# Up projection of an MLP by seven products instead of eight: 26 pairs with ordinary tiles between their chunks, in place of 40 in a row

## The chip, the cores and the metric

One core of a Trainium2 chip runs the whole program. Its engines have separate in-order queues: TensorE (PE, matmuls; PEld are its weight loads), VectorE (DVE), ScalarE (ACT), GpSimd (POOL) and SyncE (SP, which here issues all DMAs). The metric is the device time of one execution in microseconds (us); lower is better.

## The reference

A decoder block on 512 tokens of width 2048 in float32: adaLN modulation, an RWKV-7 head group beside a pooling head group, an output projection with residual, then a gated MLP with a causal conv of width 3, residual, and a final RMSNorm. The part that matters here:

```python
def _conv_ffn(h, w_up, conv_w, conv_b, w_down):
    T = h.shape[1]
    u = h @ w_up
    up = jnp.pad(u, ((0, 0), (CONV_WIDTH - 1, 0), (0, 0)))
    y = conv_b
    for j in range(CONV_WIDTH):
        y = y + conv_w[j] * up[:, j:j + T]
    val, gate = jnp.split(y, 2, axis=-1)
    return (jax.nn.silu(gate) * val) @ w_down

        x = x + gt1 * mix
        h = _rmsnorm(x, norm2_g[l]) * (1.0 + sc2) + sh2
        x = x + gt2 * _conv_ffn(h, w_up[l], conv_w[l], conv_b[l], w_down[l])
    return _rmsnorm(x, norm_f_g)
```

`w_up` is 2048 x 11264 (44 tiles of 128 value columns and 44 of gate columns), `w_down` 5632 x 2048. `gt2`, the gate of the last residual, is one of six vectors `silu(c) @ w_ada + b_ada`.

## The kernel before

Activations lie transposed: channels on the 128 partitions, 512 tokens along the row. Every float32 product is made of three matmuls in a rounded format (`mm3`, L117): weights and activations are split into a high part (a cast, on ACT) and a low part (a subtraction, on DVE, or on POOL where a call says so), and high x high, high x low and low x high add up in one PSUM bank. `split_weights` (L107) loads a piece of 512 weight columns into a `wraw` buffer (four of them), casts it into `whi` (three) and subtracts into `wlo` (three); `project` (L122) runs a whole output tile so, in four pieces for 16 tiles of input channels. PSUM has eight banks (`bank`, L788).

The order of an engine's instructions is fixed before the run by a scheduler that models their times: of what is ready it takes what stands first in the program, so later work can come ahead of earlier work that waits. `tc.issue_after(x)` holds instructions behind `x` in the queue of its engine. A tile pool closed and opened again reuses the same memory, so a new tile waits for the readers of the old ones there.

The stages around the change:

- Output projection (L848 to L875): `x2` tiles are loaded, ten output tiles get their last two input tiles, six more run in two halves of 256 tokens; after each, `residual` (L803) adds into `x2` and its squares, and a store puts `x2[f]` to DRAM (`x2d`, L856 and L863), for the end of the kernel to read back (L1020).
- First up tiles (`up_first`, L824): pairs 0 and 1 of the up projection, value and gate tile each, over 16 input tiles, in two halves of tokens, while `second_norm` still makes the activations `H2`.
- `token_sums` (L905): for the products below, four combinations of token halves and input halves for each of eight pairs of `H2` tiles, 128 x 256 each: six additions or subtractions on POOL, then two casts (L919, ACT) and two subtractions (L920, DVE) into the tiles `tk`.
- Pairs 2 and 3 (`up_tile`, L927) as ordinary tiles: 16 x 3 matmuls with 512 columns of tokens each, 96 for a pair.
- Pairs 4 to 43 (`seven`, L937): a pair is seen as a 2 x 2 block product: token halves, halves of the input channels, and value or gate. Seven products of half-size blocks replace eight: 7 x 8 x 3 = 168 matmuls with 256 columns. The eight tiles of input come in four chunks. For a chunk, 512 KB of weights (four blocks) are loaded into `raw`; POOL makes four sums of blocks (L944 to L946); `parts` (L948) splits the three plain blocks and then the four sums into `uh` and `ul` (L954 on ACT, L955 on DVE); then 42 matmuls run, products 1, 2, 4 on plain blocks first, then 6, 7, 5, 3 on the sums. Each product has its own PSUM bank through the four chunks. At the end DVE combines the seven (L981 to L988) into value and gate.
- `gated` (L838): conv of value and gate (`conv`, L831: one pass of ACT, two of DVE each), silu, product, store to `actd`.
- Gate rows (`ada_gate2`, L994): beside pairs 4 to 35, two rows a pair: a 256 KB load and a DVE product with its sum (L1002) for `gt2`, 64 in all.
- Down projection (L1043 to L1074): 44 input tiles in steps of four over eight output tiles at a time, from reloaded `actd` tiles (L1031); the second eight output tiles end in two token halves.

Of the kernel before, what the change touches and what calls it, by code (L numbers as in the profile page):

```python
# [9 lines left out]
F32 = mybir.dt.float32  # L10
# [6 lines left out]
P = 128  # L17
T = 512
# [13 lines left out]
NORD = 4  # L32
# [29 lines left out]
def block_kernel(ctx, tc, a, out, stop=None, dbg=None):  # L62
# [43 lines left out]

    def split_weights(src, eng=V):  # L107
        w = src.shape[-1]
        raw = wp.tile([P, WC], F32, tag="wraw", name="wraw", bufs=4)
        nc.sync.dma_start(raw[:, 0:w], src)  # L110
        hi = wp.tile([P, WC], F32R, tag="whi", name="whi", bufs=3)
        S.copy(hi[:, 0:w], raw[:, 0:w])  # L112
        lo = wp.tile([P, WC], F32R, tag="wlo", name="wlo", bufs=3)
        eng.tensor_tensor(lo[:, 0:w], raw[:, 0:w], hi[:, 0:w].bitcast(F32), op=ALU.subtract)  # L114
        return hi, lo
# [721 lines left out]

    def gated(j, cv, cg):  # L838
        yv, yg = conv(cv, j, "t0"), conv(cg, 44 + j, "t1")
        S.activation(yg, yg, AF.Silu)  # L840
        after = V.tensor_mul(yv, yv, yg)
        nc.sync.dma_start(actd[j], yv)
        return after
# [8 lines left out]
    for f in range(NW):  # L852
        ps = bank()
        project(ps, a["wout"][f, :, NM * P :], M[NM:])
        residual(f, ps, mod[:, 32 + f : 33 + f], acc, 0, T, f == 0)
        nc.sync.dma_start(x2d[f], x2[f])  # L856
# [32 lines left out]
    for k in range(KT):  # L889
        up_first(1, k)  # L890
    rxctx.close()
# [13 lines left out]
    def token_sums(i):  # L905
        bb = up.tile([P, 2, T], F32, tag="raw", name="bb", bufs=3)
# [3 lines left out]
        tt = up.tile([P, 2, T], F32, tag="raw", name="tt", bufs=3)  # L910
# [4 lines left out]
        G.tensor_tensor(t4, t2, bb[:, 1, 0:HT], op=ALU.subtract)  # L915
        got = []
# [7 lines left out]
    for i in range(HK):  # L924
        token_sums(i)

    def up_tile(n):  # L927
        ps = bank()
        project(ps, a["wup"][n - 4, :, :], H2)
        return ps  # L930

    for j in range(2, NORD):
        gated(j, up_tile(2 * j), up_tile(2 * j + 1))
# [3 lines left out]
    def seven(j):  # L937
        q = {}
        for c in range(NPC):
            raw = up.tile([P, 4, W2], F32, tag="raw", name="raw", bufs=3)  # L940
            nc.sync.dma_start(raw, a["wups"][j - NORD, c, :, :, :])
            sm = [wp.tile([P, WC], F32, tag="wraw", name="sums", bufs=4) for _ in range(2)]
            sa, sb2 = (t[:, :].rearrange("p (n w) -> p n w", n=2) for t in sm)
            G.tensor_tensor(sa, raw[:, 1:3, :], raw[:, 0:1, :].to_broadcast([P, 2, W2]), op=ALU.add)  # L944
            G.tensor_tensor(sb2[:, 0, :], sa[:, 0, :], raw[:, 2, :], op=ALU.add)
            G.tensor_tensor(sb2[:, 1, :], sb2[:, 0, :], raw[:, 3, :], op=ALU.add)  # L946

            def parts(srcs):  # L948
                hi = up.tile([P, 4, W2], F32R, tag="uh", name="uh", bufs=3)
                lo = up.tile([P, 4, W2], F32R, tag="ul", name="ul", bufs=3)  # L950
                got, n = [], 0
                for t in srcs:
                    m = t.shape[1]
                    S.copy(hi[:, n : n + m, :], t)  # L954
                    V.tensor_tensor(lo[:, n : n + m, :], t, hi[:, n : n + m, :].bitcast(F32), op=ALU.subtract)  # L955
                    got += [(hi[:, n + i, :], lo[:, n + i, :]) for i in range(m)]
                    n += m
                return got

            a22, a11, a12 = parts([raw[:, 1:4, :]])  # L960
            s1, s3, s2, s4 = parts([sa, sb2])

            ks = [2 * c, 2 * c + 1]
            lo = [half([H2[k], H2[k + HK]], 0) for k in ks]
            hi = [half([H2[k], H2[k + HK]], 1) for k in ks]
            for n, w, xs_ in (
                (1, a11, [x[0] for x in lo]), (2, a12, [x[1] for x in lo]),
                (4, a22, [TK[k][3] for k in ks]), (6, s2, [TK[k][1] for k in ks]),
                (7, s3, [TK[k][2] for k in ks]), (5, s1, [TK[k][0] for k in ks]),
                (3, s4, [x[1] for x in hi]),  # L970
            ):
                if c == 0:
                    q[n] = bank()[:, 0:HT]
                for i in range(2):
                    sl = slice(i * P, (i + 1) * P)
                    mm3(q[n], w[0][:, sl], w[1][:, sl], *xs_[i], start=c == 0 and i == 0, stop=c == NPC - 1 and i == 1)
# [14 lines left out]
    cbs = []  # L991
    modg = cp.tile([P, 4, KT], F32, tag="modg", name="modg")

    def ada_gate2(n, after):  # L994
        kq, j = divmod(n, KT)
        if j == 0:
            cbs.append(wp.tile([P, WC], F32, tag="whi", name="cb2", bufs=3))
            nc.sync.dma_start(cbs[kq], cact[0:1, kq * T : (kq + 1) * T].partition_broadcast(P))
        wa = wp.tile([P, WC], F32, tag="wlo", name="wa3", bufs=3)
        nc.sync.dma_start(wa, a["ada3"][kq, j, :, :])  # L1000
        with tc.issue_after(after.ins):
            V.scalar_tensor_tensor(wa, wa, 1.0, cbs[kq], op0=ALU.mult, op1=ALU.mult, accum_out=modg[:, kq, j : j + 1])  # L1002

    for j in range(NORD, NF):
        after = gated(j, *seven(j))
        for n in range(2 * (j - NORD), 2 * (j - NORD + 1)):
            if n < 4 * KT:
                ada_gate2(n, after)
    upctx.close()
    V.tensor_add(modg[:, 0, :], modg[:, 0, :], modg[:, 1, :])  # L1010
    V.tensor_add(modg[:, 2, :], modg[:, 2, :], modg[:, 3, :])
    V.tensor_add(modg[:, 0, :], modg[:, 0, :], modg[:, 2, :])
    V.tensor_add(mod[:, 80:96], modg[:, 0, :], cols("b_ada", 80, 96))
# [28 lines left out]

    pss = [bank() for _ in range(NB)]  # L1043
    for k0 in range(0, NF, DK):
        A = act_tiles(k0)
        for f in range(NB):
# [31 lines left out]
def pack(x, c, w_ada, b_ada, norm1_g, w_in, mu_shift, w0, w2, a0, a2, g2, k_k, k_a, r_k, ln_x_w, ln_x_b,  # L1078
# [49 lines left out]
    def ftiles(w):  # L1128
# [53 lines left out]
```

## Time and profile before

| | us |
|---|---|
| median of three runs (lowest, highest) | 2409.46 (2406.38, 2413.34) |
| the profiled execution | 2411.78 |
| its span in the profile | 2409.9 |
| ordinary tiles of pairs 2 and 3, first matmul to first product | 45.2 |
| pairs 4 to 43, to the first matmul of the down projection | 859.7 |

The page gives for each engine its busy time and number of instructions, and then groups of instructions by line, with busy time, the mean of one, and what ended the idle time before. PE is busy 92% of the span, but its matmuls overlap in the pipeline, so that a busy time says less than the distance from one start to the next. Other views of the same trace give busy time by stage, the waits by pair of engines, and instructions in order of time.

### The profile page before, as it was taken

Reading aid. Unit: us, or ns where it says so; the run is one execution under the profiler, and the core shown is the slowest. Engines: PE = TensorE matmul, PEld = TensorE weight load, DVE = VectorE, ACT = ScalarE, POOL = GpSimd, SP = SyncE. Lnnn points to the kernel's source line nnn. Section 1 sums busy time; section 2 is a strip of 40 time slices with the busy share of each in tenths; the row PEclk is TensorE's granted clock in tenths of the full one; section 3 lists DMA queues with packets and bytes.
Section 4 is the critical chain, followed back from the end, with each engine's and each line's share of the span. In section 5 each row is a group of like instructions: output and inputs, shape, how many; then the busy total and the mean of one; then the engine's idle time right before and its main releaser. Section 6 shows DMA issues by size and latency. Waiting matters only on the chain.

```text
span 2409.9 us, 44500 instructions
## 1 busy us (share of the span) xinstructions
PE 2212.3 (92%) x17314; PEld 1923.0 (80%) x17314; DVE 1791.8 (74%) x2686; ACT 984.0 (41%) x1621; POOL 768.8 (32%) x558
## 2 busy tenths in 40 slices
PE   7998898898789797799999999999999999999997
PEld 5786656566567697699999999999999888888887
DVE  7896667576865469679999999999988633353357
ACT  4335242332423255344444444444444433343333
POOL 0000000000000016467778777787788300000000
PEclk9998999999989899799999999999999999999999
DMA  9884555547674664334334433443333554554455
GB/s 347 296 311 161 171 171 174 178 131 235 205 233 147 205 195 143 114 132 136 129 135 136 137 136 131 137 136 135 116 118 115 182 155 144 149 149 140 141 167 177
DMA packets 188837, 400.51 MB, mean 166 GB/s; under 512 B 36561, under 2 KB 48593, under 8 KB 184401
## 3 DMA queue, kind: packets, MB, share of 16 engines
q1 hardware_dynamic: 188626, 397.68, 50.6%
q8 instruction: 135, 2.21, 0.4%
q14 instruction: 76, 0.62, 0.1%
HBM read 363.51 MB, written 34.09 MB: 165 GB/s over the span
## 4 chain that ended last, share of the span: by engine, by line
PE 69%; DVE 13%; DMA 10%; issue 3%; ACT 2%; POOL 2%; SPq 1%; DVEq 0%; ACTq 0%; POOLq 0%
PE b L120 18%; PE b L118 17%; PE b L119 17%; DMA war<-ada 5%; DVE ul L955 3%; PE mm L120 3%; PE mm L118 3%; PE mm L119 3%; PE pf L118 2%; PE pf L119 2%; PE pf L120 2%; DVE wlo L114 1%; DVE war L369 1%; DVE t L834 1%; POOL bb L909 1%
## 5 line engine op out<-in xcount | busy, mean ns | idle before, releaser
L114 DVE TENSOR_TENSOR wlo<-wraw,whi 128x512 fp32r<-128x512 f32 (+1 forms) x466 | 324.8, 699 | 317.7 <-ACT whi L112 309.4
L112 ACT CAST whi<-wraw 128x512 fp32r<-128x512 f32 (+1 forms) x482 | 290.8, 606 | 562.4 <-PE b L119 255.2
L944 POOL TENSOR_TENSOR sums<-raw 128x512 f32<-128x512 f32 x160 | 324.4, 2028 | 185.0 <-DVE ul L955 151.1
L120 PE MATMUL b<-tk,ul 128*128 128x256 f32 x1280 | 366.0, 286 | 2.6 <-DVE ul L955 2.6
L118 PE MATMUL b<-ah,whi 128*128 128x512 f32 (+1 forms) x980 | 350.3, 357 | 14.6 <-ACT whi L112 13.6
L118 PE MATMUL b<-tk,uh 128*128 128x256 f32 x1280 | 362.1, 283 | 0.0
L119 PE MATMUL b<-tk,uh 128*128 128x256 f32 x1280 | 362.0, 283 | 0.0
L120 PE MATMUL b<-ah,wlo 128*128 128x512 f32 (+1 forms) x980 | 349.5, 357 | 5.6 <-DVE wlo L114 4.7
L119 PE MATMUL b<-al,whi 128*128 128x512 f32 (+1 forms) x980 | 348.6, 356 | 0.0
L120 PE MATMUL b<-hh,ul 128*128 128x256 f32 x960 | 274.9, 286 | 37.4 <-DVE ul L955 37.4
L955 DVE TENSOR_TENSOR ul<-sums,uh 128x512 fp32r<-128x512 f32 x320 | 288.9, 930 | 18.2 <-ACT uh L954 17.4
L118 PE MATMUL b<-hh,uh 128*128 128x256 f32 x960 | 271.6, 283 | 0.0
L119 PE MATMUL b<-hl,uh 128*128 128x256 f32 x960 | 271.5, 283 | 0.0
L955 DVE TENSOR_TENSOR ul<-raw,uh 128x768 fp32r<-128x768 f32 x160 | 246.5, 1541 | 13.3 <-ACT uh L954 13.2
L120 PEld LDWEIGHTS b<-tk,ul 128*128 128x128 f32 x1280 | 245.3, 192 | 5.8 <-DVE ul L955 4.2
L118 PEld LDWEIGHTS b<-tk,uh 128*128 128x128 f32 x1280 | 245.5, 192 | 0.0
L119 PEld LDWEIGHTS b<-tk,uh 128*128 128x128 f32 x1280 | 245.4, 192 | 0.0
L954 ACT CAST uh<-sums 128x512 fp32r<-128x512 f32 x320 | 182.7, 616 | 148.2 <-PE b L119 133.3
L118 PEld LDWEIGHTS b<-ah,whi 128*128 128x128 f32 x980 | 186.2, 190 | 43.0 <-ACT whi L112 17.1
L120 PEld LDWEIGHTS b<-hh,ul 128*128 128x128 f32 x960 | 184.0, 192 | 43.9 <-DVE ul L955 43.9
L120 PEld LDWEIGHTS b<-ah,wlo 128*128 128x128 f32 x980 | 186.1, 190 | 33.6 <-DVE wlo L114 6.6
L954 ACT CAST uh<-raw 128x768 fp32r<-128x768 f32 x160 | 132.8, 830 | 193.0 <-PE b L119 193.0
(265 smaller groups left out, 4468.5 us busy)
## 6 DMA issues: line engine op xcount, KB each, us to landing
raw<-wups SPq DMA_DIRECT2D x160, 512.0 KB, 3.2
war<-ada SPq DMA_DIRECT2D x96, 512.0 KB, 4.3
wraw<-wdn SPq DMA_DIRECT2D x192, 256.0 KB, 2.9
wa<-ada SPq DMA_DIRECT2D x32, 1024.0 KB, 7.8
wraw<-win SPq DMA_DIRECT2D x108, 256.0 KB, 3.9
ald<-actd SPq DMA_DIRECT2D x88, 256.0 KB, 2.7
wraw<-wout SPq DMA_DIRECT2D x78, 256.0 KB, 3.6
wa<-ada SPq DMA_DIRECT2D x64, 256.0 KB, 2.6
```

Source lines behind the costliest of these rows:

```text
L112: S.copy(hi[:, 0:w], raw[:, 0:w])
L114: eng.tensor_tensor(lo[:, 0:w], raw[:, 0:w], hi[:, 0:w].bitcast(F32), op=ALU.subtract)
L118: PE.matmul(ps, wh, xh, start=start, stop=False)
L119: PE.matmul(ps, wh, xl, start=False, stop=False)
L120: return PE.matmul(ps, wl, xh, start=False, stop=stop)
L369: V.scalar_tensor_tensor(wa, wa, 1.0, cq[0], op0=ALU.mult, op1=ALU.mult, accum_out=modq[:, kq, j : j + 1])
L834: V.scalar_tensor_tensor(y[:, 1:T], c[:, 0 : T - 1], col("cw", 88 + j), y[:, 1:T], op0=ALU.mult, op1=ALU.add)
L909: G.tensor_tensor(bb[:, q, :], hi[:, :].bitcast(F32), lo[:, :].bitcast(F32), op=ALU.add)
L944: G.tensor_tensor(sa, raw[:, 1:3, :], raw[:, 0:1, :].to_broadcast([P, 2, W2]), op=ALU.add)
L954: S.copy(hi[:, n : n + m, :], t)
L955: V.tensor_tensor(lo[:, n : n + m, :], t, hi[:, n : n + m, :].bitcast(F32), op=ALU.subtract)
```

## The change

Pairs 2, 3 and 4 are ordinary (`NORD` 5), pairs 5 to 30 are made by seven products (`NSEV` 26), and 31 to 43 are ordinary again. The tiles of these last thirteen are cut into quarters: a quarter (four input tiles, 12 matmuls) is run in each chunk of a product pair from the third chunk on, between the products on plain blocks and those on sums. Weight sums and the split of the plain blocks are made one chunk ahead; the split of the sums is queued behind the next chunk's plain split. Buffers of `raw`, `p` and `s` parts are two each. Sums' buffers lie in the memory of `wraw` and `wlo`.

Token sums: POOL's part of four is made at once, and the casts and subtractions stand behind the last weight split of an ordinary tile, one or two sums to a tile; POOL's part of the next sum follows each. The sixteen stores of `x2` come after the first up tiles. The gate rows move into the first pass of the down projection, eight rows in each of the steps two to nine, with two buffers of rows.

```diff
-NORD = 4
+NORD = 5
+NSEV = 26
...
-        S.copy(hi[:, 0:w], raw[:, 0:w])
+        mark[0] = S.copy(hi[:, 0:w], raw[:, 0:w]).ins
...
-        eng.tensor_tensor(lo[:, 0:w], raw[:, 0:w], hi[:, 0:w].bitcast(F32), op=ALU.subtract)
+        mark[1] = eng.tensor_tensor(lo[:, 0:w], raw[:, 0:w], hi[:, 0:w].bitcast(F32), op=ALU.subtract).ins
...
         residual(f, ps, mod[:, 32 + f : 33 + f], acc, 0, T, f == 0)
-        nc.sync.dma_start(x2d[f], x2[f])
...
-        if hf:
-            nc.sync.dma_start(x2d[f], x2[f])
...
         up_first(1, k)
+    for f in range(KT):
+        nc.sync.dma_start(x2d[f], x2[f])
     rxctx.close()
...
-        bb = up.tile([P, 2, T], F32, tag="raw", name="bb", bufs=3)
+        bb = up.tile([P, 2, T], F32, tag="raw", name="bb", bufs=2)
...
-        tt = up.tile([P, 2, T], F32, tag="raw", name="tt", bufs=3)
+        tt = up.tile([P, 2, T], F32, tag=("sh", "sl")[i % 2], name="tt", bufs=2)
...
-    for i in range(HK):
-        token_sums(i)
...
+    tts = [token_sums(i) for i in range(4)]
+    at = 0
     for j in range(2, NORD):
-        gated(j, up_tile(2 * j), up_tile(2 * j + 1))
+        tiles = []
+        for i in range(2):
+            ps = bank()
+            last = project(ps, a["wup"][2 * j + i - 4, :, :], H2)
+            tiles.append(ps)
+            for _ in range((1, 1, 2, 1, 2, 1)[2 * j + i - 4]):
+                with tc.issue_after(mark[0]), tc.issue_after(mark[1]):
+                    token_split(at, tts[at])
+                at += 1
+                if at + 3 < HK:
+                    tts.append(token_sums(at + 3))
+        gated(j, *tiles)
...
+    def weight_sums(raw):
+        sa = wp.tile([P, WC], F32, tag="wraw", name="sums", bufs=4)[:, :].rearrange("p (n w) -> p n w", n=2)
+        sb2 = wp.tile([P, WC], F32, tag="wlo", name="sums", bufs=3)[:, :].rearrange("p (n w) -> p n w", n=2)
...
+    def plain_tiles():
+        for j in range(NORD + NSEV, NF):
+            yv = None
+            for i in range(2):
+                ps = bank()
+                for k0 in range(0, KT, WC // P):
+                    k1 = k0 + WC // P
+                    project(ps, a["wup"][2 * (j - NSEV) + i - 4, :, k0 * P : k1 * P], H2[k0:k1],
+                            start=k0 == 0, stop=k1 == KT)
+                    if k1 == KT:
+                        y = conv(ps, j + NF * i, f"t{i}")
+                        if i:
+                            gate_pair(j, yv, y)
+                        yv = y
+                    yield
...
+    raws = [load_four(0), load_four(1)]
+    sums = weight_sums(raws[0])
+    pw, _ = parts("p", [raws[0][:, 1:4, :]])
+    q = {}
+    for n in range(NST):
+        c = n % NPC
+        if n + 1 < NST:
+            raw = raws.pop()
+            nsums = weight_sums(raw)
+            npw, marks = parts("p", [raw[:, 1:4, :]])
+            if n + 2 < NST:
+                raws.append(load_four(n + 2))
+        with tc.issue_after(marks[0].ins), tc.issue_after(marks[1].ins):
+            sw, _ = parts("s", sums)
...
+        for m, w, xs_ in ((1, a11, b11), (2, a12, b21), (4, a22, t4)):
+            if c == 0:
+                q[m] = bank()[:, 0:HT]
+            product(q[m], c, w, xs_)
+        if n >= 2:
+            next(others, None)
+        for m, w, xs_ in ((6, s2, t2), (7, s3, t3), (5, s1, t1), (3, s4, b22)):
+            if c == 0:
+                q[m] = bank()[:, 0:HT]
+            product(q[m], c, w, xs_)
+        if c == NPC - 1:
+            gated(NORD + n // NPC, *combine(q))
+        if n + 1 < NST:
+            sums, pw = nsums, npw
+    for _ in others:
+        pass
...
+    def ada_gate2(kq, js):
+        cb = rb.tile([P, T], F32, tag="t0", name="cb2", bufs=2)
+        nc.sync.dma_start(cb, cact[0:1, kq * T : (kq + 1) * T].partition_broadcast(P))
+        for j in js:
+            wa = rb.tile([P, T], F32, tag="t1", name="wa3", bufs=2)
+            nc.sync.dma_start(wa, a["ada3"][kq, j, :, :])
+            V.scalar_tensor_tensor(wa, wa, 1.0, cb, op0=ALU.mult, op1=ALU.mult, accum_out=modg[:, kq, j : j + 1])
+
     pss = [bank() for _ in range(NB)]
     for k0 in range(0, NF, DK):
         A = act_tiles(k0)
+        n = k0 // DK
+        if 1 <= n <= 8:
+            ada_gate2((n - 1) // 2, range(8 * ((n - 1) % 2), 8 * ((n - 1) % 2) + 8))
```

More of the change, by code (lines that the diff above doesn't have):

```diff
@@ L836, in conv, with gate_pair @@
         return y
+    def gate_pair(j, yv, yg):
+        S.activation(yg, yg, AF.Silu)
+        V.tensor_mul(yv, yv, yg)
+        nc.sync.dma_start(actd[j], yv)
     def gated(j, cv, cg):
[L839 to L843, printed above, removed]
+        gate_pair(j, conv(cv, j, "t0"), conv(cg, NF + j, "t1"))
     rxctx, rx = stage("rx")
@@ L915, in token_sums, with token_split @@
         G.tensor_tensor(t4, t2, bb[:, 1, 0:HT], op=ALU.subtract)
+        return tt
+    def token_split(i, tt):
         got = []
@@ L922, in token_sums @@
         TK.append(got)
-    for i in range(HK):
-        token_sums(i)
[L927 to L930, printed above, removed]
-    for j in range(2, NORD):
-        gated(j, up_tile(2 * j), up_tile(2 * j + 1))
-    W2 = 2 * P
[L937 to L976, printed above, removed]
@@ new lines, in block_kernel, with load_four @@
+    W2 = 2 * P
+    def load_four(n):
+        raw = up.tile([P, 4, W2], F32, tag="raw", name="raw", bufs=2)
+        nc.sync.dma_start(raw, a["wups"][n // NPC, n % NPC, :, :, :])
+        return raw
+    def weight_sums(raw):
+        sa = wp.tile([P, WC], F32, tag="wraw", name="sums", bufs=4)[:, :].rearrange("p (n w) -> p n w", n=2)
+        sb2 = wp.tile([P, WC], F32, tag="wlo", name="sums", bufs=3)[:, :].rearrange("p (n w) -> p n w", n=2)
+        G.tensor_tensor(sa, raw[:, 1:3, :], raw[:, 0:1, :].to_broadcast([P, 2, W2]), op=ALU.add)
+        G.tensor_tensor(sb2[:, 0, :], sa[:, 0, :], raw[:, 2, :], op=ALU.add)
+        G.tensor_tensor(sb2[:, 1, :], sb2[:, 0, :], raw[:, 3, :], op=ALU.add)
+        return sa, sb2
@@ new lines, in parts @@
+    def parts(tag, srcs):
+        m = sum(t.shape[1] for t in srcs)
+        hi = up.tile([P, m, W2], F32R, tag=tag + "h", name=tag + "h", bufs=2)
+        lo = up.tile([P, m, W2], F32R, tag=tag + "l", name=tag + "l", bufs=2)
+        n = 0
+        for t in srcs:
+            sl = slice(n, n + t.shape[1])
+            act = S.copy(hi[:, sl, :], t)
+            dve = V.tensor_tensor(lo[:, sl, :], t, hi[:, sl, :].bitcast(F32), op=ALU.subtract)
+            n += t.shape[1]
+        return [(hi[:, i, :], lo[:, i, :]) for i in range(m)], (act, dve)
@@ L977, in seven, with product, combine @@
+    def product(q, c, w, xs_):
+        for i in range(2):
+            sl = slice(i * P, (i + 1) * P)
+            mm3(q, w[0][:, sl], w[1][:, sl], *xs_[i], start=c == 0 and i == 0, stop=c == NPC - 1 and i == 1)
+    def combine(q):
         cv = up.tile([P, T], F32, tag="cv", name="cv")
@@ L989, in seven @@
         return cv, cg
[L991 to L1008, printed above, removed]
+    def plain_tiles():
+        for j in range(NORD + NSEV, NF):
+            yv = None
+            for i in range(2):
+                ps = bank()
[9 more added lines that the diff above has]
+                    yield
@@ new lines, in block_kernel @@
+    NST = NSEV * NPC
+    others = plain_tiles()
+    raws = [load_four(0), load_four(1)]
[12 more added lines that the diff above has]
+            sw, _ = parts("s", sums)
+        (a22, a11, a12), (s1, s3, s2, s4) = pw, sw
+        ks = (2 * c, 2 * c + 1)
+        b11, b21, b22 = half([H2[k] for k in ks], 0), half([H2[k + HK] for k in ks], 0), half([H2[k + HK] for k in ks], 1)
+        t1, t2, t3, t4 = ([TK[k][i] for k in ks] for i in range(4))
+        if c == 0:
+            q = {}
+        for m, w, xs_ in ((1, a11, b11), (2, a12, b21), (4, a22, t4)):
[5 more added lines that the diff above has]
+        for m, w, xs_ in ((6, s2, t2), (7, s3, t3), (5, s1, t1), (3, s4, b22)):
+            if c == 0:
+                q[m] = bank()[:, 0:HT]
[4 more added lines that the diff above has]
+            sums, pw = nsums, npw
@@ L1041, in finish @@
         nc.sync.dma_start(out[:, k, hs], x2[k][:, hs])
+    modg = cp.tile([P, 4, KT], F32, tag="modg", name="modg")
+    def ada_gate2(kq, js):
[5 more added lines that the diff above has]
+            V.scalar_tensor_tensor(wa, wa, 1.0, cb, op0=ALU.mult, op1=ALU.mult, accum_out=modg[:, kq, j : j + 1])
     pss = [bank() for _ in range(NB)]
```

17 lines of the change are left out of this document (10 added, 7 removed).

## The prediction

> **What bounds the kernel now.** I read the page's first part, then busy time by stage, then the waits inside the stages that stand out.
>
> ```profile
> span 2409.9 us, 44500 instructions
> PE 2212.3 (92%) x17314; PEld 1923.0 (80%) x17314; DVE 1791.8 (74%) x2686; ACT 984.0 (41%) x1621; POOL 768.8 (32%) x558
> ```
>
> The profiled execution took 2411.8 us, 1.9 beyond its span and 2.3 above the median 2409.5; sums below are made against 2411.8. TensorE (PE) is busiest, so the question is where it doesn't run at its rate. The view by stages shows window, then busy time of PE, weight loads, DVE, ACT and POOL, granted clock, DMA share, GB/s:
>
> ```profile
> 939.50:996.50 57.00, 33.42 (x180) 28.77 (x179) 43.32 (x41) 20.95 (x38) 51.83 (x47) 0.76 0.24 72
> 996.50:1041.00 44.50, 44.47 (x191) 36.38 (x190) 23.93 (x35) 17.19 (x27) 9.05 (x9) 0.97 0.49 155
> ...
> 1060.00:1740.00 680.00, 643.75 (x5275) 635.75 (x5274) 680.00 (x882) 317.37 (x502) 536.99 (x375) 1.00 0.40 134
> 1760.00:1890.00 130.00, 127.36 (x1049) 125.93 (x1048) 110.13 (x153) 64.12 (x101) 107.77 (x73) 1.00 0.32 110
> 1943.00:2343.00 400.00, 400.00 (x1766) 331.20 (x1766) 166.92 (x246) 142.02 (x233) 0.00 (x0) 1.00 0.50 146
> ```
>
> Three things stand out. From 1060 to 1740, where seven-product pairs run with the gate rows beside them, DVE is busy 680 of 680 us and PE is not: DVE sets the pace. From 1760 (no gate rows) DVE falls to 85% and PE almost fills. From 939.5 to 996.5, the tail of the first up tiles, PE got through some 180 matmuls in 57 us at a clock of 0.76. The down projection (1943 on) is PE without a gap.
>
> What a matmul costs is read from the distance of starts, since the busy time of pipelined matmuls overlaps. First and last of 60 steps with 256 columns, and of 32 steps with 512:
>
> ```profile
> 1189.82 0.28 PE L118 MATMUL b<-tk,uh 128*128 128x256 f32 x1
> ...
> 1197.02 0.28 PE L118 MATMUL b<-hh,uh 128*128 128x256 f32 x1
> ```
> ```profile
> 814.64 0.39 PE L120 MATMUL b<-ah,wlo 128*128 128x512 f32 x1
> ...
> 821.89 0.39 PE L119 MATMUL b<-al,whi 128*128 128x512 f32 x1
> ```
>
> 7.20/60 = 0.120 us and 7.25/32 = 0.2266 us. So a pair by seven products is at best 168 x 0.120 = 20.16 us, an ordinary pair 96 x 0.2266 = 21.75 us. And what the stretch really took, from the first ordinary matmul over the first product to the first matmul of the down projection:
>
> ```profile
> 996.57 0.63 PE L118 MATMUL b<-hh,whi 128*128 128x512 f32 x1
> ...
> 1041.79 0.28 PE L118 MATMUL b<-hh,uh 128*128 128x256 f32 x1
> ...
> 1901.44 0.40 PE L118 MATMUL b<-ah,whi 128*128 128x512 f32 x1
> ```
>
> Forty pairs took 859.7 us, 21.49 each: of the 1.59 us that seven products save against an ordinary pair, 0.26 was left.
>
> **The change, part by part.** *Mix of pairs.* Pairs 2 to 43 were 2 ordinary and 40 by products, 904.9 us from 996.57 to 1901.44. Now they are 3 + 13 ordinary and 26 by products: 16 x 21.75 + 26 x 20.16 = 872.2 us, if PE never waits. That is 32.7 us less, although fourteen pairs lost their saving, because DVE gets room. Is there enough? The groups of 1060 to 1740 (busy us, mean ns), and the shortest, median and longest of the same operations:
>
> ```profile
> L955 DVE TENSOR_TENSOR ul<-sums,uh 128x512 fp32r<-128x512 f32 x250 | 227.1, 937 | 0.6 <-ACT uh L954 0.6
> L955 DVE TENSOR_TENSOR ul<-raw,uh 128x768 fp32r<-128x768 f32 x125 | 209.8, 1678 | 0.0
> L834 DVE SCALAR_TENSOR_TENSOR t<-cv,vec,t 128x511 f32<-128x511 f32 x32 | 38.7, 1209 | 0.0
> L835 DVE SCALAR_TENSOR_TENSOR t<-cg,vec,t 128x510 f32<-128x510 f32 x32 | 23.6, 737 | 0.0
> L986 DVE TENSOR_TENSOR cg<-b,u 128x256 f32<-128x256 f32 x32 | 13.1, 409 | 0.0
> ```
> ```profile
> L955 DVE TENSOR_TENSOR ul<-raw,uh x160: 941/1474/2049, 1006.3 to 1892.3; 128x768 fp32r<-128x768 f32 x160
> L944 POOL TENSOR_TENSOR sums<-raw x160: 1286/1741/4357, 1026.9 to 1888.1; 128x512 f32<-128x512 f32 x160
> L945 POOL TENSOR_TENSOR sums<-sums,raw x160: 733/1076/1455, 1031.3 to 1892.5; 128x256 f32<-128x256 f32 x160
> ```
> ```profile
> L1002 DVE SCALAR_TENSOR_TENSOR wa<-wa,cb x64: 674/1224/1775, 1069.3 to 1742.7; 128x512 f32<-128x512 f32 x64
> ```
>
> Take four chunks, one product pair with one ordinary tile between: PE needs 20.16 + 48 x 0.2266 = 31.0 us. DVE needs, at the stretched means, splits 4 x (1.678 + 2 x 0.937) = 14.2; four quarter-tile splits at the 1.224 of the gate rows (same size, two inputs from SBUF), 4.9; combination 7 x 0.409 = 2.9; conv 1.209 + 3 x 0.737 = 3.4; gating 0.7; the ordinary tile's conv and half a gating 1.8. Sum 27.9 of 31.0 us; at the shortest durations (0.941, 0.674, 0.737) it is some 20. The gate rows, 2 x 1.3 us a pair, are gone. POOL needs 4 x (1.29 + 2 x 0.73) = 11. So PE ends last; DVE is 65 to 90% full, and beside it the split of the sums, made late in the same chunk before, now has the quarter tile (2.7 us of PE) ahead of its use. What PE waited for:
>
> ```profile
> PE b L120 <- DVE ul L955: 36.2, 31, 1.2
> ```
> ```profile
> PE b L120 <- DVE ul L955: 2.6, 7, 0.4
> ```
>
> The first is 1060 to 1740, the second 1760 to 1890: at DVE 85% PE lost 2%. Nearest to the new load is this second row. Over 872 us bounds of 0 and 2% are 0 to 17 us of waits; with a chunk of lead I take 6. The first two chunks run without a quarter tile: 1 us more. Net gain of the mix 32.7 - 7 = 26.
>
> Here a rule bears on the room. DVE's 768-column split is 0.94 us at its shortest and 1.68 in the mean beside POOL, and L944 up to 4.36 us, so the two do hold each other up. The Trainium skill ("SBUF — State Buffer", section "SBUF: two separate sides") says DVE operations with two SBUF inputs and GpSimd operations exclude each other on a shared port for whole instructions. Worked out from the rows: a pair's two-input DVE work at its shortest (4 x 2.29 splits, 4 x 0.74 conv, 0.7 gating, 2 x 0.67 gate rows = 14.2) and POOL's 11.0 would be 25.2 us end to end; a pair took 21.5. So the trace disagrees with the rule taken strictly, by a sixth; by it four chunks of the change would fill 27 of 31 us of that port, and PE would still end last.
>
> *Token sums.* They were hoisted into the tail of the first up tiles, where ACT and DVE queued behind POOL:
>
> ```profile
> ACT tk L919 <- POOL tt L914: 29.6, 6, 5.7
> PE b L120 <- DVE wlo L114: 15.2, 12, 2.2
> PE b L118 <- ACT whi L112: 8.4, 6, 2.5
> ```
>
> ACT stood 29.6 us at casts of unfinished sums, with the weight casts of PE behind them in its queue. The 180 matmuls need 21.6 us at 0.120; they took 57, so 35 were lost, part of it to the low clock beside the gaps. Now casts and subtractions of the sums stand behind the last weight split of an ordinary tile. POOL's work stays: 51.83 us for 47 instructions, 6.6 for the six of one sum. The first four may still start under the tail and stretch DVE's weight splits there (a split has the size of the gate rows, 0.67 to 1.78 us; PE needs 12 x 0.120 = 1.44 per split); I leave 5 us of the 35 for that and take 30, bounds 20 and 35. Under six ordinary tiles (65 us of PE) eight sums take 53 us of POOL and 16 splits some 20 us of DVE, whose tiles need 4 x 0.7 of 10.9 us: hidden.
>
> *Stores of x2.* Sixteen leave the loop of the output projection. There SP held weight loads behind stores that waited for residuals:
>
> ```profile
> 820.00:840.00 20.00, 8.79 (x28) 6.28 (x27) 11.18 (x20) 6.56 (x12) 0.00 (x0) 0.66 0.91 325
> ```
> ```profile
> 824.30 5.77 SPq L856 DMA_DIRECT2D x2d<-x  x8
> 830.24 7.70 SPq L110 DMA_DIRECT2D wraw<-wout  x7
> ```
> ```profile
> ACT whi L112 <- DMA wraw<-wout: 7.1, 3, 5.6
> ```
>
> With the eight gone the loads can go out near 824, when DVE's residuals have freed their buffers; the x2 loads before them still fill the DMA engines, so I take 5 of the 6 us (bounds 0 and 8). In their new place the stores are 16 issues in front of the first ordinary weights, some 6 us of SP, and their 4 MB take some 13 us at that stage's 325 GB/s. If SP lets them out in gaps of its long weight stretch, that is free; if not, up to 8 us. I take 1.
>
> *Gate rows.* Sixty-four loads of 256 KB and 64 x 0.75 us of DVE move under the down projection, eight steps of 96 x 0.2266 = 21.75 us. DVE is 42% busy there; eight rows add 6 us of 21.75: 70%. DMA goes from 0.50 to about 0.83 (2.1 MB more in 21.75 us is 96 GB/s on top of 146), with SP in order behind two row buffers.
>
> ```profile
> wraw<-wdn SPq DMA_DIRECT2D x192, 256.0 KB, 2.9
> ```
>
> Weights run four buffers ahead, each 12 x 0.2266 = 2.7 us of PE, against 2.9 us to landing: I take 2 us, bounds 0 and 15.
>
> Sum: 26 + 30 + 5 - 1 - 2 = 58; 2411.8 - 58 = **2354 us**.
>
> **Rivals.** *DVE or the queues' fixed order stays late*: PE waits 3% of 872 us instead of 0.7%, +20: 2374. For it: stretched splits, two buffers instead of three; against: 85% DVE cost only 2% without any lead. *The gate rows collide*: SP waits for a row buffer, weights come late, 2 us in each of eight steps, +15: 2369. *The cover isn't there*: sums still starve the first up tiles, as POOL runs there either way; the 30 us stay lost: 2384. Against it: the casts, not POOL, held ACT. *Slower, by PSUM*: seven product banks and the ordinary tile's are all eight. A new tile's first quarter comes 24 + 18 matmuls, 5.0 us, after the old tile's last, and needs the old conv done: one ACT pass and two DVE passes, 0.8 + 2 x 0.74 = 2.3 us.
>
> ```profile
> L833 ACT ACTIVATE t<-cv,vec 128x512 f32<-128x512 f32 x6 | 4.9, 816 | 5.4 <-DVE cv L987 5.4
> ```
>
> If DVE puts the combination and conv of a pair (6.3 us) ahead, PE stands 3.6 us, at 26 tiles 92 us: 2446. It beats the gain only from 58/26 = 2.2 us per tile. Against it: a pair's conv falls a chunk before the tile change.
>
> **How the numbers follow.** Forecast 0.62, late DVE 0.18, colliding rows 0.07, no cover 0.07, PSUM 0.06 (of this 0.01 cancels out to no change). Range: low, no waits at all and each term at its good end: 2354 - 7 - 5 - 3 - 3 = 2336. High: the first three rivals, the last of them at 2384, and 2 us of run to run: 2386. A difference under 0.3% (7 us) can't be told from none. Faster 0.94, same 0.01, slower 0.05.
>
> **What would show it.** Between 1060 and the down projection DVE under 95% and PE over 97%; the stretch of pairs 2 to 43 near 880 us; no ACT waits on POOL before the first ordinary tile, which should start near 960; waits for wout near 824 shorter; the down projection as long as before. Wrong if matmuls of quarter tiles wait for DVE, if waits name a conv (L834, L835) ahead of a new tile, or if the down stage shows waits for its weights.

## The result, and the profile after

| | us |
|---|---|
| median after (lowest, highest of 4) | 2367.61 (2366.43, 2371.25) |
| median before, beside it (lowest, highest of 4) | 2410.36 (2406.38, 2413.34) |
| ratio, 95% interval | 0.9826 [0.9808, 0.9844] |

The changed kernel is 1.7% faster. That is inside the range, and 13.6 us above the point of 2354. The first part of the page after:

```profile
span 2365.4 us, 41904 instructions
PE 2224.0 (94%) x16306; PEld 1883.8 (80%) x16306; DVE 1512.8 (64%) x2532; ACT 924.0 (39%) x1551; POOL 404.7 (17%) x390
```

PE has hardly more to do than before, and DVE 279 us less. To see where the 44.5 us of the span went, cut both traces at the same events. In order of time, the first ordinary matmul, the first one of a product and the first one of the down projection after:

```profile
959.80 0.40 PE L121 MATMUL b<-hh,whi 128*128 128x512 f32 x1
...
1026.67 0.28 PE L121 MATMUL b<-hh,ph 128*128 128x256 f32 x1
...
1836.83 0.39 PE L121 MATMUL b<-ah,whi 128*128 128x512 f32 x1
```

With the first load of x2 (814.8 us before, 813.2 after) and the first matmul of an up tile (911.3 and 904.8) that gives five stages:

| stage | before | after | change | forecast |
|---|---|---|---|---|
| up to the first load of x2 | 814.8 | 813.2 | -1.6 | 0 |
| output projection | 96.5 | 91.6 | -4.9 | -5 |
| first up tiles, to the first ordinary matmul | 85.3 | 55.0 | -30.3 | -30 + 1 |
| pairs 2 to 43 | 904.9 | 877.0 | -27.8 | -26 |
| down projection, to the end | 508.5 | 528.6 | +20.1 | +2 |
| span | 2409.9 | 2365.4 | -44.5 | -58 |

Four stages came out within 2 us of the forecast, one 18 us above it. The view by stages after (window, busy time of PE, weight loads, DVE, ACT and POOL, clock, DMA share, GB/s) shows the same:

```profile
904.83:959.80 54.97, 50.26 (x392) 48.58 (x391) 51.63 (x71) 28.94 (x57) 40.50 (x32) 0.97 0.54 160
1060.00:1740.00 680.00, 680.00 (x4726) 637.31 (x4725) 422.35 (x667) 285.66 (x469) 272.56 (x264) 1.00 0.35 116
...
1840.00:2040.00 200.00, 183.15 (x766) 142.48 (x765) 106.29 (x229) 58.35 (x97) 0.00 (x0) 0.99 0.75 240
2040.00:2336.00 296.00, 294.94 (x1435) 249.49 (x1434) 142.77 (x227) 114.86 (x192) 0.00 (x0) 1.00 0.54 153
```

In the first row, the whole stage of the first up tiles, the clock is 0.97; the tail of that stage had 0.76 before. In the second PE is busy 680 of 680 us and DVE 62%, where DVE was busy 680 and PE 644. The third row is the early down projection with the gate rows in it: PE is at 183 of 200 us with 766 matmuls, where 200/0.2266 = 883 would fit, and the DMA share is 0.75, against 0.50 and a PE without a gap before. Once the rows are through (fourth row) the gap is gone. The waits of all engines in that stage after, 1860 to 2020 (waiting engine, releaser: us in total, times, longest):

```profile
ACT ah L143 <- DMA ald<-actd: 58.4, 21, 6.8
DVE wa L1085 <- DMA wa<-ada: 45.1, 38, 3.5
...
ACT whi L115 <- DMA wraw<-wdn: 18.0, 12, 2.8
...
PE b L123 <- DVE wlo L117: 11.5, 15, 1.5
...
PE b L121 <- ACT whi L115: 2.5, 4, 1.0
```

and those of SP's queue:

```profile
SPq L1084 <- DVE wa L1085: 57.4, 57, 3.1
```

PE waits 14.0 us for splits of weights. Behind them stand ACT, waiting up to 6.8 us at a time for activations, with the weight casts queued behind them; DVE, 45 us at rows that haven't landed; and SP, 57 us at L1084 for one of two row buffers, with weights and activations queued behind. All three are candidates for the cause, and the total doesn't say which.

### The profile page after: what moved, and what is told of

Read it like the earlier page. It is cut to its first block, busy times and chain, and to the rows that moved or that the text cites. A ratio compares the mean times of both kernels' runs of the same rounds, so it can differ in the third digit from the quotient of the medians.

```text
span 2365.4 us, 41904 instructions
## 1 busy us (share of the span) xinstructions
PE 2224.0 (94%) x16306; PEld 1883.8 (80%) x16306; DVE 1512.8 (64%) x2532; ACT 924.0 (39%) x1551; POOL 404.7 (17%) x390
## 4 chain that ended last, share of the span: by engine, by line
PE 48%; DMA 5%; DVE 2%; issue 1%; ACT 0%; SPq 0%; DVEq 0%; ACTq 0%
PE b L123 16%; PE b L121 16%; PE b L122 16%; DMA wa<-ada 2%; DMA ald<-actd 2%; DMA wraw<-wdn 1%; DVE wlo L117 1%; DVE wa L1085 0%; DVE x L1074 0%; DMA x<-x2d 0%; ACT ah L143 0%; DVE al L144 0%; ACT whi L115 0%; SPq L1054 0%; PE b L170 0%
## 5 line engine op out<-in xcount | busy, mean ns | idle before, releaser
L123 PE MATMUL b<-hh,wlo 128*128 128x512 f32 (+1 forms) x640 | 237.4, 371 | 5.5 <-DVE wlo L117 5.4
L121 PE MATMUL b<-hh,whi 128*128 128x512 f32 (+1 forms) x640 | 237.7, 371 | 0.0
L122 PE MATMUL b<-hl,whi 128*128 128x512 f32 (+1 forms) x640 | 237.2, 371 | 0.0
L122 PEld LDWEIGHTS b<-al,whi 128*128 128x128 f32 x980 | 186.5, 190 | 26.4
L123 PE MATMUL mm<-ah,wlo 128*128 128x512 f32 x444 | 186.6, 421 | 6.6 <-DVE wlo L117 6.6
L121 PE MATMUL mm<-ah,whi 128*128 128x512 f32 x444 | 185.5, 418 | 7.2 <-ACT whi L115 6.6
L122 PE MATMUL mm<-al,whi 128*128 128x512 f32 x444 | 183.8, 414 | 0.0
L123 PE MATMUL b<-tk,sl 128*128 128x256 f32 x624 | 176.7, 283 | 0.5 <-DVE sl L969 0.5
L122 PE MATMUL b<-tk,sh 128*128 128x256 f32 x624 | 176.6, 283 | 0.0
L121 PE MATMUL b<-tk,sh 128*128 128x256 f32 x624 | 176.1, 282 | 0.0
L968 ACT CAST ph<-raw 128x768 fp32r<-128x768 f32 x104 | 86.4, 831 | 164.4 <-PE b L122 157.8
L956 POOL TENSOR_TENSOR sums<-raw 128x512 f32<-128x512 f32 x104 | 137.7, 1324 | 67.9 <-DMA raw<-wups 36.3
```

The costliest lines, as they stand in the source:

```text
L121: PE.matmul(ps, wh, xh, start=start, stop=False)
L122: PE.matmul(ps, wh, xl, start=False, stop=False)
L123: return PE.matmul(ps, wl, xh, start=False, stop=stop)
L968: act = S.copy(hi[:, sl, :], t)
```

## The experiments

The time up to the first load of x2, which no experiment edits, lay between 806 and 820 us from run to run. So stages of the profiled runs are compared first, cut at the same events, and totals second. In e1, e3 and e8 the gate `gt2` is its bias alone: e1 and e8 have no gate rows, e3 loads them but leaves out their products and sums. e9 and e10 load and sum 64 of each row's 512 columns.

### What the rows cost where they are, and by what

e1 takes the rows out. e2 gives them 32 buffers in the place of two, in the memory of `H2`, which has no readers left. e3 leaves the loads and takes the work off DVE: POOL touches 16 columns of each row and so frees its buffer.

```diff
 e1_no_rows
-        if 1 <= n <= 8:
-            ada_gate2((n - 1) // 2, range(8 * ((n - 1) % 2), 8 * ((n - 1) % 2) + 8))
...
 e2_32_buffers
-            wa = rb.tile([P, T], F32, tag="t1", name="wa3", bufs=2)
+            i = (kq * KT + j) % 32
+            wa = rb.tile([P, T], F32, tag=f"h{'hl'[i // 16]}{i % 16}", name="wa3")
 e3_pool_takes
-            V.scalar_tensor_tensor(wa, wa, 1.0, cb, op0=ALU.mult, op1=ALU.mult, accum_out=modg[:, kq, j : j + 1])
+            G.tensor_tensor(wa[:, 0:16], wa[:, 0:16], cb[:, 0:16], op=ALU.mult)
...
```

> The gate rows (64 loads and products) are left out; the gate is then its bias alone. If the 20 us by which the down projection grew are all the rows' (any of the three ways below), it is back at 508 us and the total at 2367.6 - 20 = 2348. If the growth comes from elsewhere (the last tiles of the up projection, the x2 loads at its start), it stays at 2368.

> Rows land in 32 buffers (the dead H2 tiles) instead of two, so that SP never waits for one and a row has landed long before DVE comes to it. Theory DVE (its queue stands at rows that have not landed, low parts of weights behind it): 16 to 20 us back, 2350. Theory SP (SP waits for a row buffer with loads of weights and activations behind): also 16 to 20 back, 2350. Theory bandwidth (the DMA engines at 0.8 deliver weights late): nothing back or worse, 2368 to 2375.

> Same 64 loads, same two buffers, but each row is read by a 16-column multiplication on POOL (idle there) in place of DVE's product; the sums are left out and the gate is its bias. Theory DVE: DVE's queue is free, 14 to 20 us back, 2350. Theory SP: SP still waits for a row to land before each load, at most 4 us back, 2365. Theory bandwidth: as SP, 2366.

After them came two with short rows, which keep the number of loads, their order and their semaphores and cut the bytes to an eighth: e9 with two buffers, e10 with 32.

```diff
 e9_short_2
...
-            nc.sync.dma_start(wa, a["ada3"][kq, j, :, :])
+            nc.sync.dma_start(wa[:, 0:64], a["ada3"][kq, j, :, 0:64])
...
```

> Each gate row is cut to its first 64 of 512 columns (loads of 32 KB, products of 64 columns; the gate is then wrong), two buffers as in the changed kernel. Down projection, 528.6 us with full rows in two buffers, 516.0 with full rows in 32, 507.8 without rows. Theory SP (waits for a row to land hold the weights' loads, whatever the size): short loads still land in some 2 us instead of 3.6 to 4.1, so 515 to 520 and total 2355 to 2360. Theory bandwidth: 508 to 510, total 2348.

> Short rows as in the run beside it, in 32 buffers. If what 32 buffers left of the loss (516.0 against 507.8) is bytes on the DMA engines or DVE's time for the rows: 508 to 509, total 2348. If it is the number of issues in SP's queue or rows not landed in time: 512 to 516, total 2353 to 2356.

And last one with rows of full size that changes their place in SP's queue. e12 has 32 buffers as e2, but queues one row directly behind each weight tile's load, and holds its product on DVE behind the split of that tile:

```diff
 e12_spread_32
...
+        with tc.issue_after(mark[2]):
             nc.sync.dma_start(wa, a["ada3"][kq, j, :, :])
+        with tc.issue_after(mark[1]):
+            V.scalar_tensor_tensor(wa, wa, 1.0, cbs[kq], op0=ALU.mult, op1=ALU.mult, accum_out=modg[:, kq, j : j + 1])
...
+            if 1 <= n <= 8:
+                gate_row(8 * (n - 1) + f)
...
```

> From the changed kernel: each gate row is loaded right behind one down projection weight tile, one row in each step instead of in bursts, into one of 32 buffers, and its product on DVE is held behind the split of that weight tile. The bytes are the full ones. With 32 buffers and bursts the down projection took 516.0 us, with short rows 506 to 507, with the rows elsewhere 506 to 508. If the 8 to 10 us that 32 buffers left come from the bursts, in which rows stand ahead of weights and activations in the issue queue, the down projection takes 508 to 510 us here and the whole about 2348 to 2350. If they come from the bytes on the DMA engines, which are the same, it takes about 516 and the whole about 2355 to 2357. If it is longer than 520, the one product a step on DVE ahead of the next split is the cost, which neither theory names.

The down projection of each, and PE and the DMA share in 200 us of it from about 3 us after its first matmul:

| | rows | buffers | down projection, us | PE busy of 200 | matmuls | DMA | median, ratio [95%] |
|---|---|---|---|---|---|---|---|
| after | full, in groups | 2 | 528.6 | 183.2 | 766 | 0.75 | 2367.61, 0.9826 [0.9808, 0.9844] |
| e1 | none | | 507.8 | 197.1 | 863 | 0.54 | 2345.07, 0.9728 [0.9698, 0.9757] |
| e3 | full, no DVE | 2 | 528.3 | 185.6 | 766 | 0.76 | 2369.04, 0.9838 [0.9809, 0.9867] |
| e2 | full, in groups | 32 | 516.0 | 192.4 | 823 | 0.73 | 2361.01, 0.9798 [0.9759, 0.9838] |
| e9 | an eighth | 2 | 506.0 | 197.2 | 869 | 0.60 | 2343.82, 0.9737 [0.9712, 0.9763] |
| e10 | an eighth | 32 | 507.3 | 196.8 | 861 | 0.59 | 2346.95, 0.9747 [0.9724, 0.9770] |
| e12 | full, one behind each weight | 32 | 505.6 | 198.0 | 873 | 0.77 | 2349.04, 0.9770 [0.9753, 0.9787] |

**e1**: the rows cost 528.6 - 507.8 = 20.8 us. **e3**: taking the rows' work off DVE alone gives nothing back. Its view of the stage has DVE at 66 us where it was 106, and PE no better off:

```profile
1848.50:2048.50 200.00, 185.55 (x766) 146.06 (x765) 65.59 (x97) 58.50 (x97) 20.94 (x64) 0.97 0.76 240
```

But PE's waits move, 1865 to 2025:

```profile
ACT ah L143 <- DMA ald<-actd: 60.0, 24, 8.4
...
PE b L121 <- ACT whi L115: 11.0, 9, 1.9
```

PE now waits for casts of weights, which stand in ACT's queue behind activations that come late. In the changed kernel most of its wait, 11.5 of 14.0 us, was for low parts of weights, which DVE makes.

**e2**: with 32 buffers SP no longer waits for rows, and in the profiled run 12.6 of the 20.8 us come back, not all. That run is the fastest of its four, which spread from 2349.08 to 2369.70; by the medians it is 6.6 us, and the intervals of the two ratios overlap. What is left in the profiled run passes through DVE (1854 to 2014):

```profile
DVE wa L1086 <- DMA wa<-ada: 18.9, 12, 3.1
...
PE b L123 <- DVE wlo L117: 3.9, 4, 1.4
```

In all four of these waits of PE, the last thing that DVE had stood at before the split was a row that hadn't landed. So 32 buffers didn't bring what the expectation took for granted, rows that land long before DVE comes to them, and e2 doesn't rule DVE out. **e9**: with short rows everything comes back although the two buffers stayed and SP still waited at them, more than half as long as in the changed kernel:

```profile
SPq L1084 <- DVE wa L1085: 29.8, 36, 2.8
```

So a wait of SP for a row buffer isn't by itself what PE pays for; up to here the bytes seemed to be. **e12** says what about the bytes: it moves all of them at a DMA share of 0.77, the highest of all, and loses nothing, 505.6 us against 507.8 without any row. Its stage, with no wait of PE in the like 160 us:

```profile
1846.00:2046.00 200.00, 197.99 (x873) 163.31 (x872) 113.86 (x242) 66.41 (x110) 0.00 (x0) 1.00 0.77 251
```

The difference is in what stands ahead of what. SP's queue in the changed kernel, at the end of one step of the down projection (start, us with the waits inside, number of issues):

```profile
1871.26 2.01 SPq L1065 DMA_DIRECT2D ald<-actd  x2
1874.51 1.45 SPq L1084 DMA_DIRECT2D wa<-ada  x2
...
1876.52 0.86 SPq L1065 DMA_DIRECT2D ald<-actd  x2
1878.46 1.85 SPq L1084 DMA_DIRECT2D wa<-ada  x2
1880.40 2.73 SPq L113 DMA_DIRECT2D wraw<-wdn  x3
```

and ACT at the same time:

```profile
1877.01 0.62 ACT L115 CAST whi<-wraw 128x512 fp32r<-128x512 f32 x1
1881.43 1.27 ACT L143 CAST ah<-ald 128x512 fp32r<-128x512 f32 x2 [3.79 <-DMA ald<-actd]
1884.96 1.88 ACT L115 CAST whi<-wraw 128x512 fp32r<-128x512 f32 x3 [2.26 <-DMA wraw<-wdn]
```

The four activation tiles of a step go out in two parts with rows between them and after them, and the weights only behind those: ACT stands 3.79 us for the second part and 2.26 us for the weights, and casts three weight tiles at once that should have come one by one. At this place PE itself waited 0.27 us. Most of what it waited from 1860 to 2020 came by DVE's queue: in 13 of its 15 waits for low parts (10.3 of 11.5 us), the last thing that DVE had stood at before the split was a row that hadn't landed. The longest of them, on DVE and on PE:

```profile
1938.86 0.69 DVE L1085 SCALAR_TENSOR_TENSOR wa<-wa,cb 128x512 f32<-128x512 f32 x1 [3.45 <-DMA wa<-ada]
...
1939.48 0.69 DVE L117 TENSOR_TENSOR wlo<-wraw,whi 128x512 fp32r<-128x512 f32 x1
```
```profile
1940.22 0.50 PE L123 MATMUL b<-ah,wlo 128*128 128x512 f32 x1 [1.45 <-DVE wlo L117]
```

In e12 SP's queue reads:

```profile
1904.96 0.33 SPq L113 DMA_DIRECT2D wraw<-wdn  x1
1905.34 0.43 SPq L1089 DMA_DIRECT2D wa<-ada  x1
1905.82 0.43 SPq L113 DMA_DIRECT2D wraw<-wdn  x1
1906.29 0.43 SPq L1089 DMA_DIRECT2D wa<-ada  x1
...
1917.45 5.76 SPq L1065 DMA_DIRECT2D ald<-actd  x4
```

and ACT's waits for activations fall from 58.4 us and DVE's for rows from 45.1, while ACT's for weights stay near the 18.0 of the changed kernel:

```profile
ACT ah L143 <- DMA ald<-actd: 22.9, 22, 2.7
ACT whi L115 <- DMA wraw<-wdn: 18.9, 12, 2.9
...
DVE wa L1091 <- DMA wa<-ada: 1.3, 2, 0.9
```

It isn't that transfers were quicker. The landings of the changed kernel, 1845 to 2035 (number, KB, median us from issue to landing):

```profile
wraw<-wdn SPq DMA_DIRECT2D x64, 256.0 KB, 3.6
wa<-ada SPq DMA_DIRECT2D x64, 256.0 KB, 3.6
ald<-actd SPq DMA_DIRECT2D x32, 256.0 KB, 3.4
```

and of e12 in the same window:

```profile
wraw<-wdn SPq DMA_DIRECT2D x69, 256.0 KB, 4.2
wa<-ada SPq DMA_DIRECT2D x64, 256.0 KB, 4.6
ald<-actd SPq DMA_DIRECT2D x36, 256.0 KB, 2.8
```

Weights take longer in e12 and come in time; activations, with no rows between them, are quicker. The Trainium skill ("DMA: Bandwidth & Descriptors", section "Rules for kernel authors") advises to issue a transfer early and wait for it late, so that its fixed cost overlaps with work; e12 agrees, with 4.2 us per landing at no cost to PE.

What is shown: full rows in groups cost 20.8 us with two buffers, and with 32 still 8 in e2 and 13 in e11 (below); either fewer bytes or the places of e12 take the cost away. What isn't: e12 has the deeper buffers, the loads behind those of the weights and the products behind the splits of the weights all at once; none of the three was run alone with full rows but the first, in e2. By the traces both queues matter, DVE's at rows and ACT's at activations. In e9 DVE stands at rows for 41.9 us too and PE doesn't wait for a low part, so standing there isn't by itself the price either. How much of the 20.8 us each queue made stays open.

### The pairs: whose gain is it

e8 is the kernel before without its gate rows, the order of the pairs untouched. e5 is the changed kernel with the rows back in the up projection, three or four beside each of twenty product pairs, in the buffers of the combination. e6 makes all 39 pairs from 5 on by products, in the new order, so that no quarter tiles are left between the chunks.

```diff
 e8_before_no_rows
-        for n in range(2 * (j - NORD), 2 * (j - NORD + 1)):
-            if n < 4 * KT:
-                ada_gate2(n, after)
...
 e5_rows_up
...
+        if c == 0 and 1 <= n // NPC <= 20:
+            gate_rows(n // NPC - 1)
...
 e6_39_pairs
-NSEV = 26
+NSEV = 39
```

> The kernel before without its gate rows (gate is its bias alone). If the rows are what made DVE set the pace: all 40 pairs at the 20.55 us of its last eight, pairs 4 to 43 in 822 to 826 us instead of 860, total 2375. If DVE and POOL are at their limit without them too: 21.3 us or more a pair, total over 2400.

> The changed kernel with the gate rows back beside the product pairs (three or four rows in each of twenty pairs, in buffers of the combination that are free there), none under the down projection. If the rows cost time only through SP and the DMA engines under the down projection, and DVE has room beside the quarter tiles (62% busy there, 64 x 0.75 us more is 6%): down projection 508 us, pairs still near 877, total 2348. Rival: DVE and POOL hold each other up again as in the kernel before, and the rows cost 0.5 us a pair or more: pairs 890 or more, 2360 or more.

> All 39 pairs after the first three ordinary ones by seven products, no quarter tiles, gate rows still under the down projection. It asks whether the ordinary tiles were needed for DVE's room, or whether taking the rows away and making sums a chunk ahead is enough. If it is enough: 20.2 to 20.5 us a pair, three ordinary pairs 67, stretch 855 to 867 instead of 877, total 2346 to 2358. If the ordinary tiles are needed (DVE's stretched need of 21.2 us a pair decides): 39 x 21.2 + 67 = 894, total 2385.

Medians: e8 2377.11, ratio 0.9881 [0.9851, 0.9910]; e5 2357.08, 0.9788 [0.9762, 0.9813]; e6 2436.90, 1.0119 [1.0095, 1.0143]. The stretch of pairs 2 to 43, us:

| | rows beside the pairs | rows elsewhere or out |
|---|---|---|
| 40 pairs by products in a row | 904.9 (before) | 875.1 (e8), 878.0 (e11, below) |
| 26 pairs with ordinary tiles between | 882.3 (e5) | 877.0 (after), 877.7 (e1) |

Taking the rows away from the old order gives 29.8 us. The new mix on top of that gives nothing: it is 1.9 us worse than e8 and 1.0 better than e11. The new mix with the rows still there gives 22.6 us. Two remedies for one shortage of DVE, and the change paid for both. How the old order was cured, in its view of 1060 to 1740 and in what PE waited for there:

```profile
1060.00:1740.00 680.00, 667.43 (x5498) 660.99 (x5497) 571.34 (x783) 333.46 (x523) 577.79 (x393) 1.00 0.34 115
```
```profile
PE b L120 <- DVE ul L955: 12.6, 31, 0.4
```

DVE is at 84% where it was at 100%, and the wait for splits falls from 36.2 to 12.6 us: 830.9/40 = 20.77 us a pair, 0.6 above the ideal.

e6 shows what the quarter tiles are for. Without them the new order, in which the split of the sums is queued behind the next chunk's plain split, takes 879.3/39 = 22.5 us a pair, worse than before, and more than an ordinary pair:

```profile
1100.00:1800.00 700.00, 647.90 (x5202) 629.53 (x5203) 595.83 (x744) 307.40 (x496) 449.54 (x372) 1.00 0.32 106
```
```profile
ACT ph L968 <- PE b L122: 225.7, 92, 4.3
...
PE b L123 <- DVE sl L969: 52.4, 89, 1.6
```

DVE isn't full here, 85%, and PE still loses 52 us of 700 at splits of sums that come too late. The quarter tile in between (2.7 us of PE) is cover that this order needs. Two buffers of parts came with the order, where the old one had three, and ACT stands 225.7 us at casts of plain parts until PE lets go of one; what each of the two does wasn't separated. "DVE at 85% costs PE 2%" holds for one order of the queue with its buffers, and not for another.

### Token sums, stores, and the other parts with the old pairs

e7 makes the token sums early again, with their casts and subtractions where POOL's work is. e4 puts the stores of x2 back into the loop. e11 is the kernel before, with its 40 pairs in a row, and all other parts of the change, the rows in 32 buffers.

```diff
 e7_tokens_early
-    tts = [token_sums(i) for i in range(4)]
-    at = 0
+    for i in range(HK):
+        token_split(i, token_sums(i))
...
 e4_stores_back
+        nc.sync.dma_start(x2d[f], x2[f])
...
+        if hf:
+            nc.sync.dma_start(x2d[f], x2[f])
...
-    for f in range(KT):
-        nc.sync.dma_start(x2d[f], x2[f])
```

> The changed kernel with all eight token sums and their casts again in program order ahead of the ordinary tiles, held behind nothing. My step (casts of unfinished sums stand in ACT's queue ahead of weight casts): the stage from the first up tile to the first ordinary tile goes from 55 back to some 85 us, total 2395. Rival (the stage became shorter for another reason, as the stores' new place): stays near 55, total 2368.

> The stores of x2 stand after each residual again, everything else as in the changed kernel. My step (stores held weight loads behind residuals): the stage from the first x2 load to the first up tile grows from 91.6 back to about 96.5 us, total 2372. Rival (the stage became shorter for another reason, or the stores only moved the wait): no change, 2368.

> The pairs as in the kernel before (2 ordinary, 40 by seven products with three buffers, sums in the same chunk, no quarter tiles), with the other parts of the change: stores after the first up tiles, token casts behind ordinary tiles (two per tile, over four tiles), gate rows under the down projection, here in 32 buffers. If the new mix of pairs brings nothing by itself and the rows' leaving brought the pairs' gain: pairs 2 to 43 in 875 us against 877, first up tiles 55 to 58, down projection 516, total 2352. If the mix was needed as well: 890 or more for the pairs, 2367 or more.

**e7**: 2395.44, ratio 0.9947 [0.9932, 0.9962]; the first up tiles take 86.4 us, 31.4 more, and the wait of before is back (930 to 1000):

```profile
ACT tk L925 <- POOL tt L917: 21.7, 6, 4.5
```

**e4**: 2369.74, ratio 0.9838 [0.9813, 0.9863]. The totals can't tell it from the changed kernel; its output projection takes 95.7 us, 4.1 more. The stage can: it took 95.1 to 96.5 us in the three kernels with the stores in the loop (before, e8, e4) and 90.0 to 94.1 in the eleven without, in the mean 95.8 against 92.0. So the stores are worth some 4 us. PE's longest wait for a cast of weights in that stage, 7.6 us before and 1.9 after, is 6.8 in e4. **e11**: 2373.42, ratio 0.9859 [0.9828, 0.9891]. Pairs 2 to 43 take 878.0 us, near e8's 875.1, and the down projection with 32 row buffers 520.7, 4.7 more than in e2. Its first up tiles take 72.1 us rather than 55, by a wait of its own: SP stood at the first load of product weights, which goes into a buffer that POOL's token sums still used, with the weights of the ordinary tiles behind it (SP's waits, 925 to 972):

```profile
SPq L953 <- POOL tt L916: 18.9, 1, 18.9
```

So its total is no fair price for the old pairs.

### A faster version

e12 is the fastest of the kernels that leave nothing out: 0.9770 [0.9753, 0.9787] against 0.9826 [0.9808, 0.9844] for the changed kernel, each against the kernel before beside it; the intervals don't meet. From the first load of x2 to the end it takes 1532.8 us, the changed kernel 1552.2. e5, 0.9788 [0.9762, 0.9813] and 1536.4 us by the same stretch, gets nearly there the other way, and by the intervals the two can't be told apart. Forty pairs in a row with rows spread as in e12 would by the stages be as good (875.1 and 505.6) and wasn't run.

## Why the prediction came out as it did

**Mix of pairs, 26 against 27.8.** The size was right and the mechanism, DVE gets room, too. The 6 us of waits didn't come: PE waited for nothing from 1060 to 1740, DVE stood at 62%, just under the low end of "65 to 90% full", since the splits ran near their shortest. Of 877.0 us 872.2 were the ideal. What the working didn't separate is what made the room: it counted "the gate rows are gone" as one line of the mix. e8 shows that this line alone is worth the whole term, and the fourteen pairs given up for ordinary tiles gave nothing beyond it. One sum of the working is short: where it puts the DVE and POOL work of four chunks end to end, 27 of 31 us, the ordinary tile's conv and half a gating, 1.8 us, are missing. With them it is 28, and the reading, that PE ends last, stands.

**Token sums, 30 against 30.3**, shown by e7 (31.4). No wait of ACT on POOL was left between 905 and 960, the first ordinary tile started at 959.80 ("near 960"), and the 5 us left for stretched splits are there:

```profile
PE b L123 <- DVE wlo L117: 4.6, 5, 2.1
```

**Stores, 5 against 4.9** in this pair of runs, and some 4 over all runs. The scheduler put the first of the sixteen stores at 825 us, in gaps of the loop itself, and the last at 907; none stood in front of the ordinary weights, so the 1 us of their new place wasn't paid.

**Gate rows, 2 against 20.1: the step that failed.** The prediction put it so: "Weights run four buffers ahead, each 12 x 0.2266 = 2.7 us of PE, against 2.9 us to landing: I take 2 us, bounds 0 and 15." The shares that it worked out weren't exceeded (DVE 70% forecast, 53% measured; DMA 0.83 forecast, 0.75 measured), and the landings grew only to 3.6 us. What it left out is that four buffers ahead is a statement about queues: it holds only as long as SP gets to the loads, ACT to the casts and DVE to the splits. Rows in groups with two buffers, between and behind the activations of a step, take that lead away: ACT stands 58.4 of 160 us at activations with the next weight casts behind them, and DVE 45.1 us at rows that haven't landed with the next splits behind them. The prediction counted DVE by its share, and a share of 53% doesn't show that. The upper bound of 15 was too low as well: the rows' price was 20.8. The rival "the gate rows collide" at 2369 named this mechanism, put 2 us on each of eight steps, and got a chance of 0.07; measured are 20.8/8 = 2.6 us a step, and the time came out 1.4 us under it. Its cause "SP waits for a row buffer" is a part of it: in the profiled run 32 buffers give back 12.6 us, and 8 remain until the loads of the rows move behind those of the weights and their products behind the splits. Which of these two moves takes the 8 away is open.

**Rivals.** Late DVE didn't come, nor the missing cover, nor PSUM: no wait of PE named a conv between 1060 and 1800. But e6 shows that the first was one number away: with 39 pairs the same code is slower than before.

**The sum.** 44.5 us of span against 58 forecast: 18.1 by the rows, and back 1.8 by the mix, 1.3 in the first up tiles and 1.6 in stages before the change, 0.1 lost at the stores. The 1.6 are luck, since no part of the change touches those stages.

## What to carry to other kernels

When one engine is short, price each relief alone before you add two: here moving the rows or thinning the pairs each cured DVE, and the second one bought nothing. Work moved into a stage with room on every engine still has to be given a place in the issue queue: ask what is queued behind each load and how far ahead the loads of the critical chain then run, and put filler one by one behind them rather than in groups before them, its loads behind their loads and its work behind their work. And a busy share predicts waits only for the order of the queues in which it was measured.

## What the runs showed of the hardware

DVE and POOL stretched each other less than strict exclusion would, and by an amount that changed with the other work in DVE's queue. DVE's split of 768 columns had a mean of 1.678 us before and 0.995 us after; the first row below is POOL's sum in the groups of 1060 to 1740 before (busy us, mean ns), then both operations in the same stretch after:

```profile
L944 POOL TENSOR_TENSOR sums<-raw 128x512 f32<-128x512 f32 x125 | 250.6, 2005 | 121.2 <-DVE ul L955 121.2
```

```profile
L956 POOL TENSOR_TENSOR sums<-raw 128x512 f32<-128x512 f32 x88 | 115.7, 1315 | 42.6 <-DMA raw<-wups 29.3 <-DVE u L987 5.9 <-issue 3.3
...
L969 DVE TENSOR_TENSOR pl<-raw,ph 128x768 fp32r<-128x768 f32 x87 | 86.6, 995 | 128.4 <-ACT ph L968 128.4
```

In e8 POOL had the same sums to make as before, and the plain split still fell to 1.003 us there:

```profile
L955 DVE TENSOR_TENSOR ul<-raw,uh 128x768 fp32r<-128x768 f32 x131 | 131.5, 1003 | 48.9 <-ACT uh L954 48.9
```

So taking 2.6 us of gate rows from each pair took another 4 x 0.675 = 2.7 us from its plain splits, while POOL's sum went from 2.005 to 2.179 us. The Trainium skill ("SBUF — State Buffer", section "SBUF: two separate sides") says that such operations of DVE and GpSimd's shut each other out for whole instructions. By that, what the prediction worked out for a pair, 25.2 us, less two rows at their shortest (1.3), would be 23.9 us in e8; a pair took 20.77. The trace disagrees with the rule taken strictly, by 3.1 us a pair; before it was 3.7 (25.2 against 21.49).

The 256 KB loads of the down projection's weights took 2.9 us to landing before (whole run), 3.6 in the changed kernel at a DMA share of 0.75 and 4.2 in e12 at 0.77, where its rows took 4.6; in e12 PE waited for none of them.
